# Eight of the 22 gate/value pairs of a gated MLP as seven half products each, with the splits of the early gated values moved back

## The chip, the cores and the metric

The kernel runs on one core of a Trainium2 chip. The metric is device time of the whole kernel in microseconds (us). The kernel before takes 888.9 us, the median of three runs (888.84 to 888.97).

Engines: TensorE (PE; PEld is its weight load) multiplies, VectorE (DVE) and ScalarE (ACT) work element by element, GpSimd (POOL) hardly takes part, SyncE (SP) issues most of the transfers. Each engine works off its own list of instructions in the order in which the built program holds them; semaphores hold an instruction back until what it needs is there.

## The reference, cut to what matters

One decoder layer over 528 tokens (16 meta tokens and 512 others), model width 1024. Two mixers read one normalised input through a common projection, their outputs go through an output projection, and a gated MLP with 2816 hidden channels follows. The change touches the MLP:

```python
def conv_glu_ffn(h, w_up, conv_w, conv_b, w_down):
    u = causal_dwconv(h @ w_up, conv_w, conv_b)      # width 3 over tokens
    gate, val = jnp.split(u, 2, axis=-1)             # 2816 channels each
    return (jax.nn.silu(gate) * val) @ w_down

h = h + conv_glu_ffn(rmsnorm(h, norm2_w[l]), ffn_w_up[l], ffn_conv_w[l], ffn_conv_b[l], ffn_w_down[l])
y = rmsnorm(h, final_norm_w)                         # the 16 meta tokens are dropped
```

## The kernel before

Everything lies channels by tokens: a tile has 128 channels on the partitions and the tokens along the free dimension. Of the meta tokens the MLP computes the last two alone, which the convolution needs, so a row has 514 tokens (14 to 528).

**Products.** All are made from two parts of each operand: `hi` is the operand rounded by an ACT copy to the type of the fast multiply, and `lo` is the rest, a DVE subtraction. A product takes three multiplies for each 128 rows of the contraction: hi by hi, hi by lo, lo by hi. `product` (line 190) does this for two token ranges, 14 to 272 and 272 to 528, so a tile `pup` of the up-projection (eight blocks of 128 rows) is 8 x 3 x 2 = 48 matmuls with 258 or 256 columns.

**Weights.** `chunks` is the list of all weight tiles in the order of use. `weights` hands out the next, and sees to it that the two behind it are under way: a transfer into `raw` by SP (line 169), the copy to `whi` by ACT (line 160), the subtraction to `wlo` by DVE (line 161). Of each of `raw`, `whi` and `wlo` there are three buffers, handed out as they come free. A tile has 1024 columns, eight blocks of 128.

**The gated part.** There are 22 pairs: gate tile j and value tile 22 + j. Each tile goes through `conv3`: product into a PSUM pair of banks (`banks2`, two of them), a DVE multiply by the norm factor `rstd2` (line 803, out of PSUM into `fr`), an ACT pass for the first tap with bias (line 805, `fc`), and two DVE passes for the other taps (line 807). Then come the silu of the gate (ACT, line 814), the DVE multiply of both (line 816), and at once the split of the gated value `ac` into `hi` (ACT, line 819) and `lo` (DVE, line 820). The norm factor is applied behind the product, so the product's right side `u2h`, `u2l` needs no norm and the first product can start early.

**The down product** comes after: eight output tiles `pdn`, one after the other, each over all 22 gated tiles (lines 829 to 831; 66 matmuls with 512 columns). The last one is done in two halves of 256 tokens, and the final norm and the stores follow it.

**What sets the order.** A scheduler places the instructions when the program is built, by data dependencies and by priorities: `first()` (weights) and `evac()` (what empties PSUM) raise the priority of what stands inside. `tc.issue_after(x)` holds work back until x is placed. All named buffers (`slot`) come from rings by tag.

Of the kernel before, what the change touches and what calls it, by code (L numbers as in the profile page):

```python
# [54 lines left out]
def tile_block(ctx: ExitStack, tc: tile.TileContext, xT, w_in, w_dt, w_out, w_up, w_down,  # L55
# [21 lines left out]
    def bank(name):  # L77
        return px.tile([P, 512], F32, tag="px", name=name)
# [20 lines left out]
    def col(c):  # L99
        return pt[:, c:c + 1]  # L100
# [43 lines left out]
        oorder += [(j, 1), (j, 0)]  # L144
    chunks += [(("out", j, s), w_out[j][:, s * KD * P:(s + 1) * KD * P], KD) for j, s in oorder]
    for j in range(KF):
        chunks += [(("up", j), w_up[j], KD), (("up", KF + j), w_up[KF + j], KD)]
    for j in range(KD):
        chunks += [(("dn", j, k0), w_down[j][:, k0 * P:(k0 + kc) * P], kc) for k0, kc in ((0, 8), (8, 8), (16, 6))]
    wdone = {}  # L150
    wnext = [0]

    def raw_tiles(key):
        name = "_".join(map(str, key))
        return (wp.tile([P, KD * P], F32, tag="raw", name=f"raw_{name}", bufs=3),
                wp.tile([P, KD * P], F32R, tag="whi", name=f"whi_{name}"),
                wp.tile([P, KD * P], F32R, tag="wlo", name=f"wlo_{name}"))

    def split_weights(raw, hi, lo, d, eng):
        A.activation(hi[:, d], raw[:, d], AF.Copy)  # L160
        eng.tensor_tensor(lo[:, d], raw[:, d], hi[:, d].bitcast(F32), ALU.subtract)  # L161

    def ahead(n):
        while wnext[0] < min(n, len(chunks)):
            key, src, kc = chunks[wnext[0]]
            with first():
# [14 lines left out]
    def product(groups, xh, xl, t0, nk, k0=0):  # L181


        for k in range(len(xh)):
            first, last = k0 + k == 0, k0 + k == nk - 1
            for ps, (hi, lo) in groups:
                wh, wl = hi[:, k * P:(k + 1) * P], lo[:, k * P:(k + 1) * P]
                for w, x, s, e in ((wh, xh[k], first, False), (wh, xl[k], False, False), (wl, xh[k], False, last)):
                    for a0, a1 in ((t0, HALF), (HALF, NT)):
                        PE.matmul(ps[:, O + a0:O + a1], w, x[:, a0:a1], start=s, stop=e)  # L190
# [602 lines left out]
        log_exp(rstd2, parts, T0, 1.0 / DM)  # L793


    def conv3(j):
        w = weights("up", j)
        ps = banks2(f"pup{j}")
        product([(ps, w)], u2h, u2l, T0, KD)
        if j == 0:  # L800
            second_norm()
        r = slot(f"fr{j}", tag="pr")
        V.tensor_tensor(r[:, T0:], ps[:, O + T0:O + NT], rstd2[:, T0:], ALU.mult)  # L803
        c = slot(f"fc{j}", 512, tag="pr")
        A.activation(c[:], r[:, META:], AF.Identity, bias=col(C_FB + j), scale=col(C_FW + 88 + j))  # L805
        for s in (1, 2):
            V.scalar_tensor_tensor(c[:], r[:, META - s:NT - s], col(C_FW + (2 - s) * 44 + j), c[:],  # L807
                                   ALU.mult, ALU.add)
        return c

    ah, al = [], []
    for j in range(KF):
        c = conv3(j)
        silu = A.activation(c[:], c[:], AF.Silu)
        c2 = conv3(KF + j)
        V.tensor_tensor(c2[:], c2[:], c[:], ALU.mult)
        tag = ["b0"] * 4 + ["b1"] * 4 + ["m"] * 8 + ["ab"] * 2 + ["fqv"] * 2 + ["bc"] * 2
        hi, lo = slot(f"ac{j}_hi", 512, F32R, tag=tag[j]), slot(f"ac{j}_lo", 512, F32R, tag=tag[j])
        A.activation(hi[:], c2[:], AF.Copy)
        V.tensor_tensor(lo[:], c2[:], hi[:].bitcast(F32), ALU.subtract)  # L820
        ah.append(hi)
        al.append(lo)

    def down(ps, ws, d):
        for (hi, lo), k0, kc in ws:
# [8 lines left out]
    acc = slot("facc", 512, tag="pr")  # L834
    with tc.issue_after(silu.ins):
        A.preload_act_table_set(LOGS)
    for j in range(KD):
        ws = [(weights("dn", j, k0), k0, kc) for k0, kc in ((0, 8), (8, 8), (16, 6))]
        hh = hs[j]
        sq = slot(f"fsq{j}", 512, tag="u") if j else acc  # L840
        if j < KD - 1:
            ps = bank(f"pdn{j}")
            down(ps[:], ws, slice(0, 512))
            V.tensor_tensor(hh[:, META:], hh[:, META:], ps[:], ALU.add)
            A.activation(sq[:], hh[:, META:], AF.Square)
            A.activation(hh[:, META:], hh[:, META:], AF.Copy, scale=col(C_FN + j))
            if j:
                V.tensor_tensor(acc[:], acc[:], sq[:], ALU.add)
            continue
        ps, halves = {}, (0, 256)  # L850
        for d0 in halves:
            d, dh = slice(d0, d0 + 256), slice(META + d0, META + d0 + 256)
            ps[d0] = bank(f"pdn{j}_{d0}")
            down(ps[d0][:, 0:256], ws, d)
        for d0 in halves:
            d, dh = slice(d0, d0 + 256), slice(META + d0, META + d0 + 256)
            with evac():
                V.tensor_tensor(hh[:, dh], hh[:, dh], ps[d0][:, 0:256], ALU.add)
# [3 lines left out]
                PE.matmul(p[:, 0:256], ones, acc[:, d], start=True, stop=False)  # L862
# [81 lines left out]
```

## Time and profile before

| | |
|---|---|
| median of three runs | 888.9 us (888.84 to 888.97) |
| the profiled execution's own time | 888.07 us |
| its span, first to last instruction | 886.3 us |
| granted TensorE clock, mean | 0.997 |
| busy in the span: PE, DVE, ACT | 870.5, 549.2, 418.4 us |
| matmuls | 6936 |

The page of the profile gives busy time by engine, the chain of work that ended last, and groups of equal instructions with count and mean duration. A duration of a pipelined instruction can overlap with the next, so the distance from one start to the next is read from the timeline. In rows such as `pup<-u2h,whi_up` the output stands ahead of the arrow and the inputs behind it; `xN` is a count.

### The profile page before, as it was taken

Reading aid. Unit: us, or ns where it says so; the run is one execution under the profiler, and the core shown is the slowest. Engines: PE = TensorE matmul, PEld = TensorE weight load, DVE = VectorE, ACT = ScalarE, POOL = GpSimd, SP = SyncE. Lnnn points to the kernel's source line nnn. Section 1 sums busy time; section 2 is a strip of 40 time slices with the busy share of each in tenths; the row PEclk is TensorE's granted clock in tenths of the full one; section 3 lists DMA queues with packets and bytes.
Section 4 is the critical chain, followed back from the end, with each engine's and each line's share of the span. In section 5 each row is a group of like instructions: output and inputs, shape, how many; then the busy total and the mean of one; then the engine's idle time right before and its main releaser. Section 6 shows DMA issues by size and latency. Waiting matters only on the chain.

```text
span 886.3 us, 16306 instructions
## 1 busy us (share of the span) xinstructions
PE 870.5 (98%) x6936; PEld 831.2 (94%) x6936; DVE 549.2 (62%) x885; ACT 418.4 (47%) x632; POOL 8.8 (1%) x30
## 2 busy tenths in 40 slices
PE   7999999999999999999999999999999999999995
PEld 6998898999999999999999999999999999888885
DVE  6985977788667766453333377767766667423333
ACT  8628885966445444453222354444444444323221
POOL 1000000000000000000000000000000000000001
PEclk9999999999999999999999999999999999999998
DMA  7234341221222322255322233332223333233312
GB/s 249 91 115 147 104 128 58 73 72 49 72 72 57 111 73 61 72 174 149 93 89 86 93 96 95 96 96 90 83 92 94 97 95 90 83 90 106 89 43 95
DMA packets 29081, 84.65 MB, mean 96 GB/s; under 512 B 3128, under 2 KB 6712, under 8 KB 29008
## 3 DMA queue, kind: packets, MB, share of 16 engines
q1 hardware_dynamic: 26480, 80.02, 29.0%
q10 hardware_dynamic: 2528, 3.60, 1.4%
q8 instruction: 54, 0.88, 0.4%
q14 instruction: 19, 0.16, 0.1%
HBM read 81.45 MB, written 2.15 MB: 94 GB/s over the span
## 4 chain that ended last, share of the span: by engine, by line
PE 95%; DMA 2%; ACT 1%; DVE 1%; issue 0%; SPq 0%; DVEq 0%
PE pj L190 32%; PE pup L190 28%; PE pout L190 10%; PE pdn L829 5%; PE pdn L830 5%; PE pdn L831 5%; PE psy L490 1%; PE psy L493 1%; DMA x<-in_xT_dram 1%; PE psu L447 1%; PE po L709 1%; PE po L708 1%; PE pa L692 1%; PE pS L680 1%; DMA rs_d<-rh 1%; PE psx L435 1%
## 5 line engine op out<-in xcount | busy, mean ns | idle before, releaser
L190 PE MATMUL pj<-u_lo,whi_in 128*128 128x272 f32 (+1 forms) x752 | 157.1, 288 | 0.0
L190 PE MATMUL pj<-u_hi,wlo_in 128*128 128x272 f32 (+1 forms) x752 | 156.3, 286 | 0.0
L190 PE MATMUL pj<-u_hi,whi_in 128*128 128x272 f32 (+1 forms) x752 | 155.3, 287 | 0.0
L190 PE MATMUL pup<-u2h,wlo_up 128*128 128x258 f32 x704 | 141.6, 282 | 0.0
L190 PE MATMUL pup<-u2h,whi_up 128*128 128x258 f32 x704 | 140.7, 282 | 0.0
L190 PE MATMUL pup<-u2l,whi_up 128*128 128x258 f32 x704 | 140.6, 281 | 0.0
L190 PEld LDWEIGHTS pj<-u_lo,whi_in 128*128 128x128 f32 x752 | 116.2, 188 | 2.4 <-issue 1.9
L190 PEld LDWEIGHTS pj<-u_hi,wlo_in 128*128 128x128 f32 x752 | 116.5, 189 | 2.0 <-issue 1.9
L190 PEld LDWEIGHTS pj<-u_hi,whi_in 128*128 128x128 f32 x752 | 115.5, 188 | 2.4 <-issue 2.3
L190 PEld LDWEIGHTS pup<-u2l,whi_up 128*128 128x128 f32 x704 | 108.1, 189 | 0.0
L190 PEld LDWEIGHTS pup<-u2h,wlo_up 128*128 128x128 f32 x704 | 108.0, 188 | 0.1
L190 PEld LDWEIGHTS pup<-u2h,whi_up 128*128 128x128 f32 x704 | 107.6, 188 | 0.0
L161 DVE TENSOR_TENSOR wlo_in<-raw_in,whi_in 128x1024 fp32r<-128x1024 f32 (+1 forms) x58 | 64.4, 1110 | 55.5 <-ACT whi_in L160 55.3
L160 ACT ACTIVATE whi_in<-raw_in 128x1024 fp32r<-128x1024 f32 (+1 forms) x58 | 56.0, 966 | 63.9 <-PE pj L190 59.2
L829 PE MATMUL pdn<-ac_hi,whi_dn 128*128 128x512 f32 (+1 forms) x198 | 73.2, 369 | 0.0
L830 PE MATMUL pdn<-ac_lo,whi_dn 128*128 128x512 f32 (+1 forms) x198 | 73.0, 369 | 0.0
L831 PE MATMUL pdn<-ac_hi,wlo_dn 128*128 128x512 f32 (+1 forms) x198 | 72.7, 367 | 0.0
L160 ACT ACTIVATE whi_up<-raw_up 128x1024 fp32r<-128x1024 f32 x44 | 46.7, 1061 | 49.1 <-PE pup L190 32.5
L807 DVE SCALAR_TENSOR_TENSOR fc<-fr,pt,fc 128x512 f32<-128x512 f32 x88 | 65.9, 749 | 2.4 <-ACT fc L805 0.9
L161 DVE TENSOR_TENSOR wlo_up<-raw_up,whi_up 128x1024 fp32r<-128x1024 f32 x44 | 53.9, 1226 | 14.8 <-ACT whi_up L160 14.8
L161 DVE TENSOR_TENSOR wlo_dn<-raw_dn,whi_dn 128x1024 fp32r<-128x1024 f32 (+1 forms) x24 | 27.3, 1137 | 57.4 <-ACT whi_dn L160 57.4
L803 DVE TENSOR_TENSOR fr<-pup,rstd 128x514 f32<-128x514 f32 x44 | 30.5, 693 | 47.7 <-PE pup L190 43.7
(293 smaller groups left out, 1414.5 us busy)
## 6 DMA issues: line engine op xcount, KB each, us to landing
raw_in<-in_w_in_dram SPq DMA_DIRECT2D x50, 512.0 KB, 3.6
raw_up<-in_w_up_dram SPq DMA_DIRECT2D x44, 512.0 KB, 3.6
raw_out<-in_w_out_dram SPq DMA_DIRECT2D x16, 512.0 KB, 3.8
raw_dn<-in_w_down_dram SPq DMA_DIRECT2D x16, 512.0 KB, 3.6
ab<-acum_d SPq DMA_DIRECT2D x16, 264.0 KB, 4.1
raw_dn<-in_w_down_dram SPq DMA_DIRECT2D x8, 384.0 KB, 3.1
rb<-rs_d SPq DMA_DIRECT2D x8, 257.0 KB, 4.4
xr<-in_xT_dram ACTq DMA_DIRECT2D x8, 257.0 KB, 3.3
```

The lines of the kernel that those rows point to most:

```text
L160: A.activation(hi[:, d], raw[:, d], AF.Copy)
L161: eng.tensor_tensor(lo[:, d], raw[:, d], hi[:, d].bitcast(F32), ALU.subtract)
L190: PE.matmul(ps[:, O + a0:O + a1], w, x[:, a0:a1], start=s, stop=e)
L435: PE.transpose(psx[0:n, t * P:(t + 1) * P], xs[t][:, a0:a1], ident)
L447: PE.matmul(psu[:], btk[0:n, b * P:(b + 1) * P], xdc[b][0:n, :], start=True, stop=True)
L490: PE.matmul(psy[q0:q0 + 64, a0 - META:a1 - META], xdt[b][:, hc], Ls[h][:, a0:a1], start=True, stop=False)
L493: PE.matmul(psy[q0:q0 + 64, a0 - META:a1 - META], ss[b - 1][:, hc], abs_[h][:, a0:a1], start=False, stop=True)
L803: V.tensor_tensor(r[:, T0:], ps[:, O + T0:O + NT], rstd2[:, T0:], ALU.mult)
L807: V.scalar_tensor_tensor(c[:], r[:, META - s:NT - s], col(C_FW + (2 - s) * 44 + j), c[:], ALU.mult, ALU.add)
L829: PE.matmul(ps, wh, xh, start=k0 + k == 0, stop=False)
L830: PE.matmul(ps, wh, xl, start=False, stop=False)
L831: PE.matmul(ps, wl, xh, start=False, stop=k0 + k == KF - 1)
```

## The change

`KINDS` gives each of the 22 pairs a kind.

- **U** (pairs 0 to 7) works as before: product of the tokens without norm, then the DVE multiply by `rstd2`.
- **N** (pairs 8, 10, 13, 15, 18, 21) takes normed tokens `nh`, `nl` as right side, with 48 matmuls for a tile as before. The DVE multiply out of PSUM falls away; the taps read PSUM themselves.
- **W** (pairs 9, 11, 12, 14, 16, 17, 19, 20) is Strassen's scheme in Winograd's form over a pair. The 2 x 2 blocks are gate and value by the two halves of the contraction (four blocks of 128 rows each), and on the other side the halves of the contraction by two token ranges, 14 to 272 and 270 to 528. In place of eight half products there are seven, with 4 x 3 = 12 matmuls of 258 columns each: 84 matmuls for a pair, where there were 96.

For W the weight sums are made on the chip (`scheme_weights`): a pair has three entries in `chunks`, `w0` (the gate tile as it is), `w2` (s1 and s2) and `w1` (two more sums; no transfer of its own, but it also makes and splits a fourth sum `s4` of 512 columns). The products `p1`, `p2`, `p6` go into single banks, `p75` and `p43` into the bank pairs. Seven DVE and ACT instructions then build gate `sg` and value `sv` (minus its sign, so its taps come from `ntap`), and the taps follow as before, 2 x 256 tokens at a time.

The normed tokens and their sums t1 to t4 are made by `normed_tokens` behind the gates of pairs 0 to 6 (`STEPS`). The gated value is kept whole in `ac` and split later (`SPLITS`): 0 to 8 behind the gates of pairs 7 to 20, 9 to 21 behind the gate of pair 21. The first two output tiles of the down product are computed side by side, and their weight tiles are fetched in that order.

```diff
+KINDS = "UUUUUUUUNWNWWNWNWWNWWN"
+STEPS = {0: (0, 1), 1: (2,), 2: (3,), 3: (4,), 4: (5,), 5: (6,), 6: (7,)}
+SPLITS = {7: (0,), 8: (1, 2), 10: (3,), 13: (4,), 15: (5,), 18: (6,), 20: (7, 8), 21: range(9, 22)}
+HT = 258
...
+        if KINDS[j] == "W":
+            chunks += [(("w0", j), w_up[j], KD), (("w2", j), w_up[KF + j], KD), (("w1", j), None, KD)]
...
+    chunks += [dn(j, *p) for p in PARTS for j in range(2)]
+    chunks += [dn(j, *p) for j in range(2, KD) for p in PARTS]
...
+    def split_half(x, hi, lo):
+        A.activation(hi, x, AF.Copy)
+        V.tensor_tensor(lo, x, hi.bitcast(F32), ALU.subtract)
+
+    def scheme_weights(key, src):
+        kind, j = key
+        if kind == "w0":
+            sums[j] = [raw_tile(key)]
+            nc.sync.dma_start(sums[j][0][:], src)
+            hi, lo = split_tiles(key)
+            split_weights(sums[j][0], hi, lo, slice(0, 2 * HK), V)
+            return hi, lo
+        if kind == "w2":
+            rg, rv = sums[j][0], raw_tile(key)
+            nc.sync.dma_start(rv[:], src)
+            s1, s2 = slot(f"s1_{j}", 512, tag="ab"), slot(f"s2_{j}", 512, tag="ab")
+            V.tensor_tensor(s1[:], rv[:, 0:HK], rv[:, HK:], ALU.add)
+            V.tensor_tensor(s2[:], s1[:], rg[:, 0:HK], ALU.add)
+            sums[j] += [rv, s2]
+            hi, lo = split_tiles(key)
+            split_half(s1[:], hi[:, 0:HK], lo[:, 0:HK])
+            split_half(s2[:], hi[:, HK:], lo[:, HK:])
+            return hi, lo
+        rg, rv, s2 = sums.pop(j)
+        V.tensor_tensor(rv[:, 0:HK], rv[:, 0:HK], rg[:, 0:HK], ALU.add)
+        V.tensor_tensor(rg[:, HK:], rg[:, HK:], s2[:], ALU.add)
+        hi, lo = split_tiles(key)
+        split_weights(rv, hi, lo, slice(0, 2 * HK), V)
+        h4, l4 = slot(f"s4h_{j}", 512, F32R, tag="ab"), slot(f"s4l_{j}", 512, F32R, tag="ab")
+        split_half(rg[:, HK:], h4[:], l4[:])
+        return hi, lo, h4, l4
...
+    def normed_tokens(i):
+        k = i // 2
+        if i % 2 == 0:
+            for kk in (k, k + KD // 2):
+                t = slot(f"n{kk}", tag="z")
+                V.scalar_tensor_tensor(t[:, T0:], hs[kk][:, T0:], col(C_N2 + kk), rstd2[:, T0:], ALU.mult, ALU.mult)
...
+                split_half(t[:, T0:], hi[:, T0:], lo[:, T0:])
...
+        V.tensor_tensor(t1, b11, b12, ALU.subtract)
+        V.scalar_tensor_tensor(t2, b22, -1.0, t1, ALU.mult, ALU.subtract)
+        V.tensor_tensor(t3, b22, b12, ALU.subtract)
+        V.scalar_tensor_tensor(t4, t2, -1.0, b21, ALU.mult, ALU.subtract)
+        for n, t in enumerate((t1, t2, t3, t4)):
+            d = slot(f"t{n + 1}_{k}", 2 * HT, F32R)
+            split_half(t, d[:, 0:HT], d[:, HT:])
...
+        hi, lo = weights("w0", j)
+        mul(p1, hi[:, 0:HK], lo[:, 0:HK], b11)
+        mul(p2, hi[:, HK:], lo[:, HK:], b21)
+        hi, lo = weights("w2", j)
+        mul(p6, hi[:, HK:], lo[:, HK:], t2)
+        mul(p75[:, 512:512 + HT], hi[:, 0:HK], lo[:, 0:HK], t1)
+        hi, lo, h4, l4 = weights("w1", j)
+        mul(p75[:, 0:HT], hi[:, 0:HK], lo[:, 0:HK], t3)
+        mul(p43[:, 512:512 + HT], h4, l4, b22)
+        mul(p43[:, 0:HT], hi[:, HK:], lo[:, HK:], t4)
+        with evac():
+            A.activation(sg[:, A_], p1, AF.Copy)
+            V.tensor_tensor(sv[:, A_], sg[:, A_], p6, ALU.add)
+            V.tensor_tensor(sg[:, A_], sg[:, A_], p2, ALU.add)
+            V.tensor_tensor(by_halves(su), sv[:, A_].unsqueeze(1).broadcast_to([P, 2, HT]), two(p75), ALU.add)
+            V.tensor_tensor(sv[:, B_], su[:, A_], p75[:, 512:512 + HT], ALU.add)
+            V.tensor_tensor(sv[:, A_], su[:, A_], p43[:, 0:HT], ALU.add)
+            V.tensor_tensor(sg[:, B_], su[:, B_], p43[:, 512:512 + HT], ALU.add)
...
+        for i in SPLITS.get(j, ()):
+            with tc.issue_after(gate.ins):
+                split_half(acs[i][:], hi[:], lo[:])
...
+    pdn = [bank(f"pdn{j}") for j in range(2)]
+    for k0, kc in PARTS:
+        w2 = [weights("dn", j, k0) for j in range(2)]
+        for k in range(kc):
+            for ps, (hi, lo) in zip(pdn, w2):
+                PE.matmul(ps[:], wh, ah[k0 + k][:], start=k0 + k == 0, stop=False)
+                PE.matmul(ps[:], wh, al[k0 + k][:], start=False, stop=False)
+                PE.matmul(ps[:], wl, ah[k0 + k][:], start=False, stop=k0 + k == KF - 1)
```

Three places of the built program, where the scheduler's order counts. The first is PE's list where pair 9 ends and pair 10 begins. Before, the last matmuls of value tile 31 (= 22 + 9) and the first of gate tile 10:

```order
L190 MATMUL pup31_7098<-u2l7_5864,whi_up_31_6965 128x256
L190 MATMUL pup31_7098<-u2h7_5863,wlo_up_31_6966 128x258
L190 MATMUL pup31_7098<-u2h7_5863,wlo_up_31_6966 128x256
L190 MATMUL pup10_7164<-u2h0_5086,whi_up_10_7031 128x258
L190 MATMUL pup10_7164<-u2h0_5086,whi_up_10_7031 128x256
```

The same place now, at the end of the seventh product of pair 9:

```order
L940 MATMUL p43_9_7145<-t4_3_6874,whi_w1_9_7153 128x258
L941 MATMUL p43_9_7145<-t4_3_6874,wlo_w1_9_7154 128x258
L939 MATMUL p1_11_7404<-n0_hi_6009,whi_w0_11_7275 128x258
L940 MATMUL p1_11_7404<-n0_lo_6010,whi_w0_11_7275 128x258
L939 MATMUL p2_11_7405<-n4_hi_6015,whi_w0_11_7275 128x258
L940 MATMUL p2_11_7405<-n4_lo_6016,whi_w0_11_7275 128x258
L250 MATMUL pup10_7279<-n0_hi_6009,whi_up_10_7186 128x258
```

Four matmuls of pair 11 now stand ahead of pair 10; they read `whi_w0_11`, which gets the buffer of `whi_w1_9`. Four matmuls of pair 19 stand ahead of pair 18 in the same way, and two of `pdn0` ahead of pair 21.

The second place is DVE's list where pair 17 (a W) ends. Before, pair 17 looked like every pair; this is pair 11's stretch, from the emptying of its gate tile on:

```order
L803 TENSOR_TENSOR fr11_7341<-pup11_7292,rstd2_5870 128x514
L161 TENSOR_TENSOR wlo_up_34_7350<-raw_up_34_7348,whi_up_34_7349 128x1024
L807 SCALAR_TENSOR_TENSOR fc11_7343<-fr11_7341,pt_75,fc11_7343 128x512 x2
L803 TENSOR_TENSOR fr33_7403<-pup33_7354,rstd2_5870 128x514
L161 TENSOR_TENSOR wlo_up_13_7416<-raw_up_13_7414,whi_up_13_7415 128x1024
L807 SCALAR_TENSOR_TENSOR fc33_7405<-fr33_7403,pt_75,fc33_7405 128x512 x2
L816 TENSOR_TENSOR fc33_7405<-fc33_7405,fc11_7343 128x512
```

Now, the end of pair 17:

```order
L966 TENSOR_TENSOR sv17_8212<-sg17_8211,p6_17_8208 128x258
L902 SCALAR_TENSOR_TENSOR fc38_8077<-sv16_8074,ntap_5871,fc38_8077 128x512
L179 TENSOR_TENSOR wlo_up_18_8252<-raw_up_18_8250,whi_up_18_8251 128x1024
L967 TENSOR_TENSOR sg17_8211<-sg17_8211,p2_17_8207 128x258
L988 TENSOR_TENSOR ac16_8204<-fc38_8077,fc16_8076 128x512
L179 TENSOR_TENSOR wlo_up_40_8282<-raw_up_40_8280,whi_up_40_8281 128x1024
L968 TENSOR_TENSOR su17_8213<-sv17_8212,p75_17_8209 128x516
L202 TENSOR_TENSOR s1_19_8400<-raw_w2_19_8398 128x512
L969 TENSOR_TENSOR sv17_8212<-su17_8213,p75_17_8209 128x258
```

The last instruction that reads `p75_17`, whose bank pair the next product `pup18` takes, stands behind two weight splits and behind `s1_19`, the first sum of a pair two further on, which waits for a transfer.

The third place is PE's list at the change to the down product. Now, around pair 21's first matmuls:

```order
L941 MATMUL p43_20_8611<-t4_3_6874,wlo_w1_20_8620 128x258
L1019 MATMUL pdn0_8922<-ac0_hi_7002,whi_dn_0_0_8748 128x512
L1020 MATMUL pdn0_8922<-ac0_lo_7003,whi_dn_0_0_8748 128x512
L250 MATMUL pup21_8753<-n0_hi_6009,whi_up_21_8652 128x258
L250 MATMUL pup21_8753<-n0_hi_6009,whi_up_21_8652 128x256
```

Two matmuls of the down product's first tile moved ahead of the last pair; they read `whi_dn_0_0`, which gets the buffer of `whi_w1_20`.

More of the change, by code (lines that the diff above doesn't have):

```diff
@@ L165, in ahead @@
             key, src, kc = chunks[wnext[0]]
+            if key[0] in ("w0", "w1", "w2"):
+                with first():
+                    wdone[key] = scheme_weights(key, src)
+                wnext[0] += 1
+                continue
             with first():
@@ L797, in conv3, with taps, at, taps_of @@
+    def taps(c, r, j, w, b):
+        n = c.shape[-1]
+        def at(s):
+            return r[..., 2 - s:2 - s + n] if len(r.shape) == 2 else r[:, :, 2 - s:2 - s + n]
+        A.activation(c, at(0), AF.Identity, bias=b, scale=w[2])
+        for s in (1, 2):
+            V.scalar_tensor_tensor(c, at(s), w[2 - s], c, ALU.mult, ALU.add)
+    def taps_of(j):
+        return [col(C_FW + i * 2 * KF + j) for i in range(3)]
+    def conv3(j, kind):
         w = weights("up", j)
         ps = banks2(f"pup{j}")
-        product([(ps, w)], u2h, u2l, T0, KD)
+        if kind == "U":
+            product([(ps, w)], u2h, u2l, T0, KD)
+        else:
+            product([(ps, w)], nh, nl, T0, KD)
@@ L800, in conv3 @@
         if j == 0:
             second_norm()
[L802 to L803 removed]
+        r = ps[:, O + T0:O + NT]
         c = slot(f"fc{j}", 512, tag="pr")
[L805 to L808, printed above, removed]
@@ L841, in tile_block @@
         if j < KD - 1:
-            ps = bank(f"pdn{j}")
-            down(ps[:], ws, slice(0, 512))
+            if j > 1:
+                ps = bank(f"pdn{j}")
+                down(ps[:], ws, slice(0, 512))
+            else:
+                ps = pdn[j]
             V.tensor_tensor(hh[:, META:], hh[:, META:], ps[:], ALU.add)
```

104 lines of the change are left out of this document (84 added, 20 removed).

## The prediction

> **What bounds the kernel now.** I read the page first, its busy times and the chain that ended last.
>
> ```profile
> span 886.3 us, 16306 instructions
> PE 870.5 (98%) x6936; PEld 831.2 (94%) x6936; DVE 549.2 (62%) x885; ACT 418.4 (47%) x632; POOL 8.8 (1%) x30
> PE 95%; DMA 2%; ACT 1%; DVE 1%; issue 0%; SPq 0%; DVEq 0%
> ```
>
> PE is the chain for 95% of the span. Next the chain in order of time from the gated part on (start, length, what), and the busy time by engine in that stretch (PE, PEld, DVE, ACT, POOL, then clock, DMA share, GB/s):
>
> ```profile
> 500.89 6.19 PE pup L190 x52
> 507.08 0.87 PE psn L791 x4
> 507.94 244.91 PE pup L190 x2060
> ...
> 867.61 0.86 PE psn L862 x4
> 508.00:752.85 244.85, 244.85 (x2061) 244.85 (x2060) 171.93 (x214) 111.51 (x136) 0.00 (x0) 1.00 0.30 93
> ```
>
> The 2112 matmuls of the gated part run without a hole to 752.85; 2060 in 244.91 us is 0.1189 us for each. So every matmul taken out there is worth 0.119 us, for as long as PE stays the last to be ready. DVE is busy 172 of 245 us, ACT 112. What fills them, by group (count | busy us, mean ns | idle before, released by):
>
> ```profile
> L807 DVE SCALAR_TENSOR_TENSOR fc<-fr,pt,fc 128x512 f32<-128x512 f32 x86 | 64.4, 749 | 2.4 <-ACT fc L805 0.9
> L161 DVE TENSOR_TENSOR wlo_up<-raw_up,whi_up 128x1024 fp32r<-128x1024 f32 x42 | 51.5, 1226 | 11.4 <-ACT whi_up L160 11.4
> L803 DVE TENSOR_TENSOR fr<-pup,rstd 128x514 f32<-128x514 f32 x44 | 30.5, 693 | 47.7 <-PE pup L190 43.7 <-ACT rstd L131 2.9
> L820 DVE TENSOR_TENSOR ac_lo<-fc,ac_hi 128x512 fp32r<-128x512 f32 x21 | 14.5, 692 | 14.1 <-ACT ac_hi L819 14.0
> L858 DVE TENSOR_TENSOR xr<-xr,pdn 128x256 f32<-128x256 f32 x2 | 0.8, 422 | 6.7 <-PE pdn L831 6.7
> L160 ACT ACTIVATE whi_up<-raw_up 128x1024 fp32r<-128x1024 f32 x42 | 44.6, 1061 | 40.9 <-PE pup L190 32.5 <-PE pout L190 4.6 <-issue 3.7
> L805 ACT ACTIVATE fc<-fr,pt 128x512 f32<-128x512 f32 x43 | 35.1, 816 | 1.1 <-DVE fr L803 1.1
> L814 ACT ACTIVATE fc<-fc 128x512 f32<-128x512 f32 x22 | 13.9, 632 | 41.3 <-DVE fc L807 41.3
> ```
>
> The weight copy on ACT waits 32.5 us for PE: it waits for a weight buffer that PE still reads. That wait is harmless while two other weight tiles are ready; it matters below.
>
> A row's duration is not what it costs in a queue. The timeline of DVE (start, length) shows starts closer together than the lengths, where an instruction does not read what the one ahead wrote:
>
> ```profile
> 330.36 0.69 DVE L642 TENSOR_TENSOR pp<-q,rq 128x512 f32<-128x512 f32 x1
> 330.97 0.68 DVE L645 TENSOR_TENSOR qS<-q,sd 128x512 f32<-128x512 f32 x1
> 331.57 0.55 DVE L646 TENSOR_TENSOR kS<-k,sd 128x384 f32<-128x384 f32 x1
> 332.03 0.42 DVE L656 TENSOR_TENSOR qBC<-q,sd 128x256 f32<-128x256 f32 x1
> 332.37 0.42 DVE L657 TENSOR_TENSOR kBC<-k,sd 128x256 f32<-128x256 f32 x1
> ...
> 639.61 1.23 DVE L161 TENSOR_TENSOR wlo_up<-raw_up,whi_up 128x1024 fp32r<-128x1024 f32 x1 [0.16 <-ACT whi_up L160]
> 640.76 1.53 DVE L807 SCALAR_TENSOR_TENSOR fc<-fr,pt,fc 128x512 f32<-128x512 f32 x2
> 642.32 0.69 DVE L816 TENSOR_TENSOR fc<-fc,fc 128x512 f32<-128x512 f32 x1
> ```
>
> Start to start: 0.60 for 512 elements (length 0.69), 0.34 for 256 (0.42), 1.15 for 1024 (1.23). Two taps that depend on each other take 1.56, so 0.78 each; two that don't I put at 0.75 - 0.08 = 0.67 (the 0.08 is what the others gain).
>
> **What is removed.** A W pair has 84 matmuls for 96, so 8 x 12 = 96 fewer: 96 x 0.1189 = 11.4 us off PE. The 672 left in W pairs have 258 columns where the mean was 257: 672 x 0.1189 / 257 = 0.3 back. Net 11.1. N and U pairs and the down product keep their matmuls.
>
> **What DVE gets.** No transfer is added or taken away (`w1` has none); SP's list only follows the new order. The three small products for `ntap` stand among the first instructions of the kernel, on a DVE that waits for transfers there. Tile by tile, for a W pair: four sums of 512, three splits of 512 (two in w2, one in s4), two splits of 1024, five TT (tensor-tensor instructions) of 258 and one of 516 out of PSUM, four taps (two and two alternate, 0.70 on the mean) and the gate product: 7 x 0.60 + 2 x 1.15 + 5 x 0.34 + 0.61 + 4 x 0.70 + 0.60 = **12.2 us**. PE takes 84 x 0.119 = 10.0 for it. An N pair has no `fr`: 2 x 1.15 + 4 x 0.72 + 0.60 = **5.8 us** (PE 11.4). Each late split adds 0.60. The operand forms with 2 x 258 and a repeated input are in no row of before; I take them by L803 and L858, which also read PSUM, since size is all that sets those lengths. The lowest price is these starts; the highest the full lengths (rivals).
>
> So the work comes in four blocks, each from an N pair to the W ahead of the next N: 10-12, 13-14, 15-17, 18-20. DVE against PE: 5.8 + 2 x 12.2 + 0.6 = 30.8 against 31.4 us; 18.6 against 21.4 for 13-14. DVE fits, with 2% to spare in three blocks of four, and ACT (about 7 us for a W by L160, L805, L814 and halves of them) with more. The point where lateness counts is the end of a block: N's first product needs the bank pair of `p75`, which was full only 2.9 us earlier (the 24 matmuls of `p43`).
>
> **The U part.** The norming of the tokens adds 2 x (0.67 + 0.60) or 4 x 0.34 + 4 x 0.34 for a step, 2.5 to 2.7 us. By the order a pair has 9 to 13 us of DVE work against 11.4, about 79 against 91 over pairs 0 to 7. A product may be emptied 5.7 us late before PE stops, since two bank pairs alternate. Taken as 0; if that cover were gone, the worst pair (0 to 1, some 2 us over) would cost 2.
>
> **Waits at the ends of blocks**, by walking the queues with the starts above:
>
> - Pairs 9 to 10, and 20 to 21. The hoisted matmuls need a `whi` whose buffer PE frees with its last matmul of the pair; behind it comes the ACT copy of 1024. How such a copy and its reader follow each other:
>
> ```profile
> 644.23 1.06 ACT L160 ACTIVATE whi_up<-raw_up 128x1024 fp32r<-128x1024 f32 x1 [0.55 <-PE pup L190]
> 645.32 1.23 DVE L161 TENSOR_TENSOR wlo_up<-raw_up,whi_up 128x1024 fp32r<-128x1024 f32 x1 [0.16 <-ACT whi_up L160]
> ```
>
> 1.06 and some 0.1 for the two hand-overs: 1.2 us each, with the whole next product queued behind. 2.4 together. (DVE alone would hold pair 10 up for 0.4, inside this.)
> - Pairs 12 to 13. The taps of pair 11 wait for an ACT queue that first copies `p1_12`, which is done 72 matmuls, 8.6 us, before the block's end, at 22.8. The copy of 258 (0.4, taken as two thirds of L814's 512) and the tap pass (0.8) end at 24.1 with the hand-over. From there DVE has four taps, two splits of 1024, two TT of 258, the gate product, `su` and the reader of `p75_12` left: 4 x 0.67 + 2 x 1.15 + 2 x 0.34 + 0.60 + 0.61 + 0.42 = 7.3, so 31.5, and 31.6 for PE, against 31.4: 0.2.
> - Pairs 14 to 15 and 17 to 18. `s1` of a later pair stands ahead of that reader and waits for its weights, whose raw buffer came free with the split `wlo_up_15` (17.1 us into a block of 21.4) or `wlo_up_18` (28.5 of 31.4). The transfer takes 3.6 us from issue to landing:
>
> ```profile
> raw_up<-in_w_up_dram SPq DMA_DIRECT2D x44, 512.0 KB, 3.6
> ```
>
> 17.1 + 3.7 + 0.6 + 0.5 = 21.9, so 0.6 late; 28.5 + 3.7 + 0.6 + 0.4 = 33.2, so 1.8 late (the hoist of `p1_19`, 1.2, lies inside).
>
> Sum of the waits: 2.4 + 0.2 + 0.6 + 1.8 = **5.0 us**. Lower bound 0, upper bound 14 (the second rival).
>
> **The hand-over to the down product.** It starts with tiles 0 to 8, which are split by then. The two output tiles side by side take 6 x 0.218 = 1.3 us for each gated tile (0.218: 114.8 us from 752.85 to 867.61 for 528 matmuls of 512 columns, the last tile's 132 halves counted as 66). Tile 9 is needed 11.7 us after the last up-matmul. DVE and ACT have its split about 5.4 us after it (one ACT tap pass, two taps, gate, split), then one split each 0.65. The weight tile `dn_1_8` can only come when PE has freed a buffer, but PE's list has 16 matmuls of `pdn0` (3.5 us) in that place. Taken as 0; with the cover gone it is a copy and a split, 1.06 + 1.23 = 2.3.
>
> **Sum.** 888.07 - 11.1 + 5.0 = 882.0 for a profiled execution; that one lay 0.8 under the median, so **882.8 us**, 0.7% faster.
>
> **Rivals.**
>
> *Nothing waits.* PE's list keeps going because the hoists find their weights. For it: PE never stood still for a weight in the stretch above. Against: there a copy had two further tiles as cover; here the buffer is read by the matmul just ahead. 888.9 - 11.1 = 877.8.
>
> *DVE becomes the bound: slower.* Place: the three blocks with two W. If each DVE instruction costs its full length there, a W has 7 x 0.69 + 2 x 1.23 + 5 x 0.42 + 0.69 + 4 x 0.75 + 0.69 = 13.8 us, an N 6.2, a block 34.5 against 31.4: 3 x 3.1 = 9.3 lost. Waits for ACT and transfers inside DVE's queue then add to the time instead of hiding (0.5 a block, 2.0), the first boundary 1.3, and the late gate of pair 21 and the down weights some 2: 14.6, so 888.9 - 11.1 + 14.6 = 892.4. It decides from some 0.08 us more for each of the 46 instructions of a block. Against it stand the starts 0.60 apart; for it, that most instructions in the new order wait for another engine, and a waiting one gains nothing from the overlap.
> A rule of the Trainium skill speaks for this rival (VectorE: DVE Perf Modes, section "The DRAIN you can't avoid"): after each operation the pipe is flushed, and the next does not start until it is empty. By that rule the blocks would go by full lengths, and the sum would be 892.4. The trace differs as far as it goes: 512 elements start 0.60 apart with rows of 0.69.
>
> *The raw buffers are the bound.* A W holds two of the three raw buffers until its last sums, so each W's second transfer starts late. If it lands 0.6 us later than 3.6 at each of eight W pairs, with a DVE queue that stands still, 5 us more: 888. For it, the two boundaries above; against, that 16 engines are at a 0.30 share.
>
> **Chances.** Forecast, with waits of 2 to 8 us (880 to 886): 0.58. Nothing waits: 0.08. Raw buffers or other waits of 8 to 12 us (886 to 890): 0.20. DVE bound: 0.14. A measurement here tells some 0.2% (1.8 us) from no change: faster means under 887.1, slower over 890.7. Faster: 0.58 + 0.08 + 0.08 of the 0.20 = 0.74. Same: the other 0.12 and 0.02 of the DVE case = 0.14. Slower: 0.12. The range 879.5 to 890.5 leaves out about 0.06 below and 0.12 above. Since few of the cases are slower, no second range is needed; the forecast's own is 880 to 886.
>
> **What would show it.** Right: 6840 matmuls; PE idle of 1 to 2 us at the five block ends and none inside; gated part of 251.9 - 11.1 + 5.0 = about 246 us; PE waits there named by `whi_w0`, `whi_dn` or `p75`. Wrong: PE idle in every W pair with DVE at over 95% busy between pairs 9 and 20 (DVE bound); holes on DVE ahead of `s1` behind a transfer (raw buffers); PE idle between 752 and 765 (hand-over); idle in U pairs.

## The result

The changed kernel takes **882.15 us** in the median of four runs (882.03 to 883.05), the kernel before 888.87 us (888.73 to 888.97). The ratio is 0.9929, with a 95% interval from 0.9918 to 0.9941: 0.7% faster. The forecast was 882.8 us.

The profiled execution of the changed kernel is the slowest of its four, 883.05 us. Its totals, and the shares of the chain that ended last:

```profile
span 880.9 us, 16283 instructions
PE 861.5 (98%) x6840; PEld 821.5 (93%) x6840; DVE 596.4 (68%) x1012; ACT 438.7 (50%) x688; POOL 8.9 (1%) x30
PE 96%; ACT 1%; DMA 1%; DVE 1%; issue 1%; DVEq 0%; SPq 0%; ACTq 0%
```

There are 96 matmuls fewer and 127 DVE instructions more. PE is busy 9.0 us less and the span is 5.4 us shorter, so PE now stands still for longer than it did. The waits of PE at the ends of W pairs, by what ended them (us in total, times, longest), and the two stretches that matter (PE, PEld, DVE, ACT, POOL, clock, DMA share, GB/s):

```profile
PE p L939 <- ACT whi_w L178: 2.1, 2, 1.1
PE pdn L1019 <- ACT whi_dn L178: 1.1, 1, 1.1
```

```profile
501.76:748.10 246.34, 243.16 (x2025) 242.11 (x2024) 216.05 (x331) 130.35 (x186) 0.00 (x0) 1.00 0.31 94
600.00:746.00 146.00, 142.82 (x1185) 141.88 (x1184) 132.25 (x203) 75.82 (x108) 0.00 (x0) 1.00 0.33 99
```

The gated part lasts 246.3 us. Where the pairs of kind W lie, DVE is busy 91% of the time (132.25 of 146.00), and PE misses 3.2 us of the stretch. The chain of waits shows where those lie (start, length, what):

```profile
508.98 96.56 PE pup L250 x812
615.52 1.06 ACT whi_w L178
617.38 11.42 PE pup L250 x96
648.50 11.56 PE pup L250 x96
670.17 11.62 PE pup L250 x96
701.91 1.07 ACT whi_w L178
703.76 11.42 PE pup L250 x96
734.87 1.07 ACT whi_dn L178
736.71 11.42 PE pup L250 x96
```

The 812 matmuls ahead of the first scheme pair run without a hole. Three times the chain goes through an ACT copy of about 1.06 us, at the ends of pairs 9, 17 and 20, and in each case the matmuls behind it are hoisted ones of a later product. One of them in the timelines of PE, ACT and DVE:

```profile
701.66 0.28 PE L941 MATMUL p<-t,wlo_w 128*128 128x258 f32 x1
703.02 0.38 PE L939 MATMUL p<-n_hi,whi_w 128*128 128x258 f32 x1 [1.08 <-ACT whi_w L178]
...
701.91 1.06 ACT L178 ACTIVATE whi_w<-raw_w 128x1024 fp32r<-128x1024 f32 x1 [3.26 <-PE p L940]
...
702.24 0.69 DVE L202 TENSOR_TENSOR s<-raw_w 128x512 f32<-128x512 f32 x1 [0.87 <-DMA raw_w<-in_w_up_dram]
702.85 0.42 DVE L969 TENSOR_TENSOR sv<-su,p 128x258 f32<-128x258 f32 x1
```

PE's last matmul of pair 17 starts at 701.66. The copy for the hoisted product waits for the buffer that this pair still reads, and PE starts again at 703.02, so 1.24 us are lost beside the usual 0.12. At the same time DVE stood still for 0.87 us ahead of the first weight sum of pair 19 (L202), whose transfer had not landed, with the reader of the bank `p75` (L969) queued behind it. That reader ended at 703.27: a second wait beside the first. It cost nothing here, since the first matmul of `pup18`, which needs that bank, stands behind the four hoisted ones and started at 703.60.

### The profile page after: what moved, and what is told of

It is laid out like the page before. It is cut to its first block, busy times and chain, and to the rows that moved or that the text cites. A ratio compares the mean times of both kernels' runs of the same rounds, so it can differ in the third digit from the quotient of the medians.

```text
span 880.9 us, 16283 instructions
## 1 busy us (share of the span) xinstructions
PE 861.5 (98%) x6840; PEld 821.5 (93%) x6840; DVE 596.4 (68%) x1012; ACT 438.7 (50%) x688; POOL 8.9 (1%) x30
## 4 chain that ended last, share of the span: by engine, by line
PE 96%; ACT 1%; DMA 1%; DVE 1%; issue 1%; DVEq 0%; SPq 0%; ACTq 0%
PE pj L250 33%; PE pup L250 18%; PE pout L250 10%; PE pdn L1006 3%; PE pdn L1007 3%; PE pdn L1005 3%; PE p L939 3%; PE p L940 3%; PE p L941 3%; PE pdn L1019 1%; PE pdn L1021 1%; PE pdn L1020 1%; PE psy L550 1%; DMA x<-in_xT_dram 1%; PE psy L553 1%; PE pa L752 1%
## 5 line engine op out<-in xcount | busy, mean ns | idle before, releaser
L178 ACT ACTIVATE whi_dn<-raw_dn 128x1024 fp32r<-128x1024 f32 (+1 forms) x24 | 23.6, 987 | 73.8 <-PE pdn L1006 53.4
L1006 PE MATMUL pdn<-ac_lo,whi_dn 128*128 128x512 f32 (+1 forms) x154 | 55.9, 363 | 0.0
L1005 PE MATMUL pdn<-ac_hi,whi_dn 128*128 128x512 f32 (+1 forms) x154 | 55.6, 361 | 0.0
L250 PE MATMUL pup<-u2h,wlo_up 128*128 128x258 f32 (+1 forms) x256 | 51.6, 283 | 0.0
L250 PE MATMUL pup<-u2l,whi_up 128*128 128x258 f32 (+1 forms) x256 | 51.1, 281 | 0.0
L250 PE MATMUL pup<-u2h,whi_up 128*128 128x258 f32 (+1 forms) x256 | 51.1, 282 | 0.0
L179 DVE TENSOR_TENSOR wlo_up<-raw_up,whi_up 128x1024 fp32r<-128x1024 f32 x28 | 34.2, 1220 | 9.8 <-ACT whi_up L178 9.7
L179 DVE TENSOR_TENSOR wlo_out<-raw_out,whi_out 128x1024 fp32r<-128x1024 f32 x16 | 19.6, 1225 | 30.1 <-ACT whi_out L178 30.1
L250 PEld LDWEIGHTS pup<-u2h,wlo_up 128*128 128x128 f32 x256 | 39.3, 188 | 0.1
L250 PEld LDWEIGHTS pup<-u2l,whi_up 128*128 128x128 f32 x256 | 39.3, 189 | 0.0
```

The source lines that it names most:

```text
L1005: PE.matmul(ps, wh, xh, start=k0 + k == 0, stop=False)
L1006: PE.matmul(ps, wh, xl, start=False, stop=False)
```

## The account of PE

Each kernel below can be followed by one sum. I take the stretch from the start of the last `psn` matmul ahead of the gated part to the start of the last `pdn` matmul, so that the work upstream, which differs by up to 2 us between single executions, is left out. The kernel before has 368.71 us there. A pair of kind W takes off 12 matmuls of 0.1189 us, and its 84 matmuls, all of 258 columns, start 0.1201 us apart (164 from 628.64 to 648.22 in the changed kernel), which gives 84 x 0.0012 = 0.10 us back: 1.33 us net. The waits are what PE's starts lie apart beyond 0.119 us, wherever they are over 0.19 apart; starts at a lower clock are in it. In the four kernels where two matmuls of `pdn0` still stand ahead of pair 21 (changed, e3, e7, e11), 0.2 us of it is no wait: these two have 512 columns and take 0.22 us each.

| kernel | W pairs | median us | ratio, 95% | waits us | 368.71 - 1.33 a pair + waits | stretch measured |
|---|---|---|---|---|---|---|
| before | 0 | 888.87 | | 0 | 368.7 | 368.71 |
| changed | 8 | 882.15 | 0.9918 to 0.9941 | 4.44 | 362.5 | 362.37 |
| all N (e6) | 0 | 888.65 | 0.9992 to 1.001 | 0 | 368.7 | 368.71 |
| no hoist (e1) | 8 | 882.65 | 0.9922 to 0.9952 | 4.61 | 362.7 | 362.64 |
| first sum held (e11) | 8 | 883.90 | 0.9938 to 0.9963 | 5.51 | 363.6 | 363.30 |
| no hoist, first sum held (e2) | 8 | 880.48 | 0.9893 to 0.9923 | 2.47 | 360.5 | 360.43 |
| the same and late taps (e9) | 8 | 880.19 | 0.9893 to 0.9920 | 2.56 | 360.6 | 360.58 |
| late taps alone (e3) | 8 | 882.68 | 0.9919 to 0.9944 | 4.45 | 362.5 | 362.37 |
| no hoist, 1 DVE add a pair (e4) | 8 | 883.07 | 0.9925 to 0.9955 | 5.60 | 363.7 | 363.64 |
| no hoist, 3 DVE adds a pair (e5) | 8 | 896.23 | 1.0065 to 1.0099 | 18.78 | 376.8 | 376.84 |
| eleven W (e7) | 11 | 893.18 | 1.0034 to 1.0062 | 19.83 | 373.9 | 373.82 |
| e9 with nine W, one early | 9 | 883.63 | 0.9928 to 0.9955 | 7.35 | 364.1 | 363.90 |
| e9 with nine W, three in a row | 9 | 882.49 | 0.9917 to 0.9947 | 5.57 | 362.3 | 362.52 |

Sum and measurement agree within 0.3 us in all of them. This is bookkeeping: the excess of the starts is read from the same trace as the stretch. What it tests is the 1.33 us of a W pair, and that no other loss lies in the stretch. So two things make the difference between these kernels: the number of matmuls, and how far PE's starts are held up, nearly always at the ends of W pairs (in e7 inside them too, and in e5, e7 and one of e10 by a lower clock as well). The experiments ask what sets that second number.

## The experiments

**The side parts alone (e6).** The scheme is not used; the normed tokens, the splits behind gates, the side by side start of the down product and the negated taps stay.

```diff
-KINDS = "UUUUUUUUNWNWWNWNWWNWWN"
+KINDS = "UUUUUUUUNNNNNNNNNNNNNN"
```

> All fourteen pairs 8 to 21 with the products of the kernel before (no pair by the scheme), with the rest of the change left in: the gated values split behind gates, the negated taps at the start. 96 matmuls come back, so by the prediction's sum the time is before + 0.3 = 888.8 us, and PE has no wait over 0.2 us at the ends of pairs 9, 12, 14, 17 and 20. If the side parts of the change cost more than the forecast gave them, 889.5 or more; if moving the splits of the gated values is worth time by itself, 888.0 or less.

Measured: 888.65 us, ratio 1.0001 (0.9992 to 1.001), and no wait of PE in the stretch. The moved splits and the normed products are worth nothing and cost nothing; DVE has room for them. In the stretch that took 132.25 us of DVE above, it needs:

```profile
600.00:746.00 146.00, 146.00 (x1230) 146.00 (x1229) 81.14 (x98) 54.70 (x69) 0.00 (x0) 1.00 0.31 94
```

**The hoists (e1).** Theory: the matmuls that the scheduler hoists ahead of an ordinary product, behind a weight copy, cost PE 1.2 us at three places. The edit holds them behind the last matmul of the pair before:

```diff
+        with tc.issue_after(last[0].ins):
             mul(p1, hi[:, 0:HK], lo[:, 0:HK], b11)
             mul(p2, hi[:, HK:], lo[:, HK:], b21)
...
+                with tc.issue_after(last[0].ins):
                     PE.matmul(ps[:], wh, ah[k0 + k][:], start=k0 + k == 0, stop=False)
```

> The change with one thing undone: the four matmuls of pairs 11 and 19 and the two of the down product that the scheduler had put ahead of pairs 10, 18 and 21 stay in their place behind those pairs. My theory (three waits of 1.2 us for a weight copy behind a matmul just ahead): at pairs 9 to 10 the 1.3 us wait falls to about 0.4 (the last reader of p75_9 ends 0.4 us after the last matmul of pair 9), at 20 to 21 from 1.3 to about 0.1; at 17 to 18 nothing is won, since the last reader of p75_17 ends 1.6 us after PE is done. Together 1.9 us: 880.2. Rival, DVE as the bound: the waits only change their name, 881.8 to 882.3. Rival, all three waits vanish: 878.5.

Measured: 882.65 us, no gain. The waits of PE of this kernel (`sv L971` is the reader of `p75`, `L969` in the changed kernel), and DVE at the end of pair 12:

```profile
PE pup L251 <- DVE sv L971: 3.5, 3, 1.7
```

```profile
647.33 0.69 DVE L970 TENSOR_TENSOR su<-sv,p 128x516 f32<-128x516 f32 x1
648.88 0.69 DVE L202 TENSOR_TENSOR s<-raw_w 128x512 f32<-128x512 f32 x1 [0.86 <-DMA raw_w<-in_w_up_dram]
649.49 0.41 DVE L971 TENSOR_TENSOR sv<-su,p 128x258 f32<-128x258 f32 x1
```

The copies no longer stop PE. The waits at the ends of pairs 9 and 20 fell as expected (1.19 to 0.48 and 1.24 to 0.18 beside the usual 0.12), but others came in their place. At the ends of pairs 12 and 17 PE's starts lie 1.75 and 1.96 us apart (0.20 and 1.36 before the edit), since the order of DVE moved as well: now the first sum of pair 14 stands ahead of the reader at the end of pair 12 and waits 0.86 us there for its transfer. My 880.2 was wrong, because it took DVE's order as given: the edit moved a stalled sum to a place where there had been no wait.

**Both, and the first sum alone (e2, e11).** The second edit holds the first weight sum of a pair behind the reader of `p75` of the W pair before it:

```diff
+                if emptied[0] is not None:
+                    st.enter_context(tc.issue_after(emptied[0]))
                 V.tensor_tensor(s1[:], rv[:, 0:HK], rv[:, HK:], ALU.add)
...
-            V.tensor_tensor(sv[:, B_], su[:, A_], p75[:, 512:512 + HT], ALU.add)
+            emptied[0] = V.tensor_tensor(sv[:, B_], su[:, A_], p75[:, 512:512 + HT], ALU.add).ins
```

> As the kernel without the hoists, and in addition the first sum s1 of a W pair is placed on DVE only behind the last reader of the p75 ahead of it, so that its wait for the weight transfer holds up nothing else. My theory (the wait at pairs 17 to 18 is s1's transfer, 0.9 us of DVE idle, and what follows it): another 1.3 us, 878.9, with 0.5 us of waits at block ends in all. Rival, the raw buffers are the bound: s1 and what hangs on it comes later still, and PE waits for w2 instead inside the W pairs: 880 or above.

> The changed kernel with the first weight sum held behind the first reader of the last bank of the pair before; the hoisted matmuls stay. Theory (the three hoists cost PE 1.3 us each whatever VectorE does, as their copy comes behind the last matmul of the pair): 882.2, no gain, PE's waits still named by the weight copies. Rival (the stalled sum was what held the ends of the blocks up, and the second run's gain came from it alone): 880.5.

Measured: 880.48 us with both. The theory had 878.9 with 0.5 us of waits; 2.5 us are left, and none of it inside a W pair, where the rival had put it. The second alone takes 883.90 us, which is no gain (its interval reaches that of the changed kernel). PE's waits in the stretch, first with both, then with the second alone:

```profile
PE pup L255 <- DVE sv L975: 1.7, 3, 0.6
```

```profile
PE p L943 <- ACT whi_w L178: 2.1, 2, 1.1
PE pdn L1023 <- ACT whi_dn L178: 1.1, 1, 1.1
PE p L945 <- DVE wlo_w L179: 0.5, 1, 0.5
PE pup L254 <- DVE sv L973: 0.2, 1, 0.2
```

By place (distance of PE's starts at the end of the pair, less 0.12):

| end of pair | changed | no hoist (e1) | first sum held (e11) | both (e2) |
|---|---|---|---|---|
| 9 | 1.19 | 0.48 | 0 | 0 |
| 12 | 0.08 | 1.63 | 1.19 | 0.63 |
| 14 | 0.12 | 0.11 | 0.33 | 0 |
| 17 | 1.24 | 1.84 | 1.24 | 0.75 |
| 20 | 1.24 | 0.18 | 1.24 | 0.78 |

At the end of pair 17 each of the two causes hides the other: the stalled sum alone leaves a wait of 1.84 us, the copy alone 1.24, and only without both does it fall to 0.75. At the other ends the single edits gained nothing for another reason: the scheduler made a new order. In e1 the stalled sum of pair 14 moved ahead of the reader at the end of pair 12; in e11 the hoist left the end of pair 9 and came up at the end of pair 12, with 0.7 us more behind it for the split of the same weights. Both edits together take the waits from 4.4 to 2.5 us. What is left is the wait for the reader of `p75` itself, 0.6 to 0.8 us at the ends of pairs 12, 17 and 20, with no transfer ahead of it. A tap pass of an earlier tile stands between it and the instruction ahead of it in the evacuation, and takes 0.67 us of DVE; no run moves that pass (DVE at the end of pair 17, with both edits):

```profile
698.96 0.69 DVE L974 TENSOR_TENSOR su<-sv,p 128x516 f32<-128x516 f32 x1
699.56 0.75 DVE L907 SCALAR_TENSOR_TENSOR fc<-sv,ntap,fc 128x512 f32<-128x512 f32 x1
700.23 0.42 DVE L975 TENSOR_TENSOR sv<-su,p 128x258 f32<-128x258 f32 x1
```

**How full DVE is (e4, e5).** On top of e1, one or three DVE additions of 512 elements that nothing needs are made in each W pair:

```diff
             V.tensor_tensor(sg[:, B_], su[:, B_], p43[:, 512:512 + HT], ALU.add)
+            for _ in range(3):
+                V.tensor_tensor(su[:, 0:512], sg[:, 0:512], sv[:, 0:512], ALU.add)
```

> As the kernel without the hoists, with one more DVE addition of 512 elements (0.60 us from start to start; its result is not used) in each W pair, right behind the emptying of the products. My theory, 30.8 us of DVE work against 31.4 of PE in three blocks and 18.6 against 21.4 in one: one addition makes 32.0, so about 0.6 us lost in three blocks, 1.8 us over the kernel without hoists (882.0). DVE as the bound: each of the eight counts in full, 4.8 us more (885.0). DVE with much room: no change (880.2).

> The same with three additions in each W pair. My theory: a block has 34.4 us of DVE work against 31.4, three blocks lose 3.0 each, the block of pairs 13 and 14 (20.4 against 21.4) nothing: 9 us over the kernel without hoists (889.2). DVE as the bound: 24 x 0.6 = 14.4 us more (894.6). DVE with much room: under 3 us (883).

Measured: 883.07 us with one. That is not told apart from e1's 882.65; in the traces the waits rise by 1.0 us (5.60 against 4.61), where the theory had 1.8. With three it is 896.23 us, more than any of the three theories gave. What an added instruction costs in DVE's queue, and PE's waits:

```profile
641.99 0.68 DVE L975 TENSOR_TENSOR su<-sg,sv 128x512 f32<-128x512 f32 x1
642.60 0.41 DVE L968 TENSOR_TENSOR sv<-sg,p 128x258 f32<-128x258 f32 x1
642.93 0.74 DVE L903 SCALAR_TENSOR_TENSOR fc<-sg,pt,fc 128x512 f32<-128x512 f32 x1
643.59 0.74 DVE L903 SCALAR_TENSOR_TENSOR fc<-sv,ntap,fc 128x512 f32<-128x512 f32 x1
644.25 0.68 DVE L975 TENSOR_TENSOR su<-sg,sv 128x512 f32<-128x512 f32 x1
```

```profile
PE pup L251 <- DVE sv L971: 11.2, 4, 4.2
```

The addition is 0.68 us long and the next starts 0.61 us after it; the readers of PSUM start 0.33 and the taps 0.66 us apart. Those are the prices of the forecast. Three blocks at 30.8 + 2 x 3 x 0.60 = 34.4 us of DVE against 31.4 of PE should lose 9.0 us; the idle time of PE at the ends of the blocks came to 12.0 us against 4.2 in e1, so 7.8 more. (Where PE ran slower, DVE had more time, so 7.8 is not a clean test of the 9.0.) The rest of the excess, 6.8 us, is no wait at all: with each wait of 3 us or more PE's clock fell. In e5 the windows that begin with those three waits' ends:

```profile
615.20:618.00 2.80, 2.80 (x24) 2.80 (x24) 2.80 (x6) 2.08 (x3) 0.00 (x0) 1.00 0.38 149
651.15:653.86 2.71, 2.71 (x12) 2.71 (x13) 2.71 (x6) 1.52 (x2) 0.00 (x0) 0.50 0.03 6
710.02:714.90 4.88, 4.88 (x23) 4.88 (x24) 4.88 (x10) 2.15 (x3) 0.00 (x0) 0.50 0.00 0
747.06:753.00 5.94, 5.94 (x28) 5.94 (x29) 5.77 (x10) 2.67 (x4) 0.00 (x0) 0.50 0.29 88
```

Behind a wait of 0.60 (the first row) the clock is 1.00 and 24 matmuls start in 2.80 us. Behind starts 4.44, 4.28 and 3.04 us apart it is 0.50, and 12 matmuls start in 2.71 us. Half of 2.71 + 4.88 + 5.94 is 6.8 us. The windows end up to 0.6 us ahead of the clock's rise, so the agreement is good to some 0.5 us.

**More W pairs (e7, and e10 on top of e9).** Eleven in two long rows; nine with one at the end of the first part; nine with three in a row:

```diff
-KINDS = "UUUUUUUUNWNWWNWNWWNWWN"
+KINDS = "UUUUUUUUNWWWWWNWWWWWWN"    (e7)
+KINDS = "UUUUUUUUWWNWWNWWNWWNWN"    (e10, early)
+KINDS = "UUUUUUUUNWWNWWNWWNWWWN"    (e10, late)
```

> Eleven pairs by the scheme instead of eight (9 to 13 and 15 to 20), 36 more matmuls off: 4.3 us more off PE. Theory (VectorE is nearly full in a block of scheme pairs, 12.2 us for a pair against 10.0 of PE): the two blocks need 67.4 and 79.6 us of VectorE against 61.4 and 71.4 of PE, so PE waits about 14 us in all; 888.5 - 15.7 + 0.3 + 14.2 = 887.3, and up to 892 if the waits are over 3 us each and the granted clock falls to half after them as it did in the run with three more additions. If VectorE is not what sets the end of a block: 888.5 - 15.7 + 5.1 = 877.9.

> On top of the three edits, nine pairs by the scheme in blocks of two with one ordinary pair between (8, 9, 11, 12, 14, 15, 17, 18 and 20): 12 more matmuls off, 1.4 us by the mean, 1.3 by the 0.1201 us that a matmul of 258 columns takes. Theory (a block of two scheme pairs and an ordinary one just fits VectorE, 30.8 us against 31.4): 880.2 - 1.3 + one more end of a block at 0.8 = about 879.7, if pair 8 finds its weight sums ready at the end of the first part. Rival (VectorE has no room left): more than 882, with waits inside the pairs.

> On top of the three edits, nine pairs by the scheme (9, 10, 12, 13, 15, 16, 18, 19 and 20): the last block has three of them in a row. Theory (three in a row need 5.8 + 3 x 12.2 + 0.6 = 43.0 us of VectorE against 41.4 of PE): that block waits some 1.6 us more, so 880.2 - 1.3 + 1.6 = 880.5. Rival (VectorE does not set the ends of the blocks): 878.9.

Measured: 893.18, 883.63 and 882.49 us, where I had expected 887.3 (up to 892), 879.7 and 880.5; all three are slower than the eight pairs that they start from. For e7, PE's waits and the stretch:

```profile
PE p L939 <- ACT whi_w L185: 4.8, 4, 1.6
PE p L941 <- DVE s4l L186: 2.9, 2, 1.6
PE p L939 <- DVE sv L969: 2.5, 5, 0.8
```

```profile
600.00:757.00 157.00, 143.02 (x1144) 139.66 (x1143) 149.59 (x241) 81.00 (x120) 0.00 (x0) 0.99 0.31 92
```

DVE is busy 95% of the stretch and PE waits inside the pairs: this is what the slower rival of the prediction was to look like, here by more work for DVE and not by a higher price of an instruction. The waits are some 18 us where I had 14.2, and one stretch at a lower clock is added. In e10 late the third W pair in a row costs 3.0 us more waits than e9 (1.6 expected), in e10 early the end of pair 9 alone makes PE's starts lie 3.31 us apart, with the lower clock behind it. In that wait DVE is busy all the time:

```profile
614.16:617.47 3.31, 0.28 (x4) 0.10 (x2) 3.31 (x6) 1.06 (x1) 0.00 (x0) 1.00 0.50 139
```

It is also busy for the whole of the 14.16 us ahead of it (from 600.00), so there nothing but its own work held it up, and it has no room for a ninth pair. In e10 late it is busy 31.53 of the 31.70 us from 703.30 to the block's end at 735.00, but 2.10 us of idle time behind an ACT copy lie just ahead of 703.30; how much of the 3.0 us comes from that, the runs don't separate.

**The negated taps (e3, e9).** They are made behind the gate of pair 1 instead of at the start.

> The three negations of the taps are made behind the gate of pair 1 instead of ahead of the first work. Theory (they stand in VectorE's list ahead of v_lo at the start, and PE's first products come 0.5 us later): 0.5 us less than the changed kernel, 881.7. If the negations are hidden as the prediction said: 882.2.

> The hoisted matmuls held behind the previous pair, the first weight sum held behind the first reader of the last bank of the pair before, and the negated taps made behind the gate of pair 1. By the sum of the runs so far: 880.5 - 0.5 = 880.0; if the negations cost nothing 880.5; if the gain of the second edit was chance, 882.

Measured: 882.68 us (no gain) and 880.19 us (the same as e2). I had taken them for the reason that the first products of the profiled execution come 0.5 us later. The chain at the start says what it was, in the kernel before and in the changed one:

```profile
5.29 4.12 DMA x<-in_xT_dram
```

```profile
5.30 4.62 DMA x<-in_xT_dram
```

A transfer that both kernels have took 0.5 us longer in that execution. The negations are hidden, as the prediction said.

e2 and e9 are the best versions of all: 0.9908 and 0.9907 of the time before (0.9893 to 0.9920 for e9), 1.7 to 2.0 us below the changed kernel. Their intervals touch that of the changed kernel (from 0.9918), but the slowest run of both (881.32) is below its fastest (882.03), and the waits in the traces are 2 us less.

## Why the prediction was right

**The bound.** Every matmul taken out was worth its distance while PE was the last to be ready; the account above closes within 0.3 us. The net of the matmuls was forecast at 11.1 us and is 8 x 1.33 = 10.6: matmuls of 258 columns lie 0.1201 us apart, not 0.1189 x 258 / 257 = 0.1194. That term was mis-sized by 0.5.

**Waits at the block ends.** None lay inside a pair, and those at pairs 9, 17 and 20 were where they were put. The forecast's sign, 1 to 2 us of PE idle at all five ends, held at these three alone; at pairs 12 and 14 there was next to none. Their sizes, measured as the distance of starts less 0.12:

| end of pair | forecast | measured | released by |
|---|---|---|---|
| 9 | 1.2 | 1.19 | copy of the hoisted product |
| 12 | 0.2 | 0.08 | |
| 14 | 0.6 | 0.12 | |
| 17 | 1.8 | 1.24 | copy; the stalled first sum beside it |
| 20 | 1.2 | 1.24 | copy for the down product |

With 0.6 us for the first matmuls behind a wait, which start 0.19 to 0.24 us apart, the waits are 4.4 us; the forecast had 5.0. Where the forecast was too high is the transfer of the first sum: the step "17.1 + 3.7 + 0.6 + 0.5 = 21.9, so 0.6 late" did not occur at the end of pair 14, and at the end of pair 17 the sum did wait (0.87 us), but PE's next matmuls were the hoisted ones, which the copy held; when they were through, the reader behind the sum had ended. The two misses, 0.5 too much gain and 0.6 too much waiting, took each other back. That is luck in part. Of the 5.0 us of waiting, the 2.4 at pairs 9 and 20 came out right in size and for the reason given; the 1.8 at pair 17 was given to the late transfer, with the hoist inside it, and it was the other way round; the 0.6 at pair 14 did not come. That the late transfer is real shows in e1, where it costs 1.84 us at pair 17 once the hoist is gone.

**The first part and the hand-over.** Taken as 0, and they are: 812 matmuls without a hole, and PE goes from the last up product into the down product at 748.12 with the starts of a normal sequence. The stretch from there to the last `pdn` is not longer than before (122.9 us against 123.4, of which 0.4 are the two matmuls done ahead of pair 21).

**The rivals.** *Nothing waits* (877.8) did not happen; the nearest that any run came is 880.2, with 2.6 us of waits left. *Raw buffers* (888) was wrong as a bound, but its mechanism is in DVE's waits in the changed kernel between pairs 9 and 21: three times ahead of a first sum, 2.2 us in all.

```profile
DVE s L202 <- DMA raw_w<-in_w_up_dram: 2.2, 3, 1.0
```

*DVE becomes the bound* (892.4) is wrong for this change and right close beside it: one more W pair is enough to lose against eight, and three more, or 1.8 us more of DVE in each, are enough to be slower than the kernel before. Its place was named rightly. Its size, 0.08 us more for each of 46 instructions of a block (3.7 us), is what e5 added (3.6 us more, slower than before); with a third of that, in e4 (1.2 us more in a block), 1.0 us was lost in all. The paragraph of the Trainium skill that spoke for it (VectorE: DVE Perf Modes, section "The DRAIN you can't avoid") also says that a next operation that is not held starts earlier, and the forecast had told its first half alone. The traces agree with that second half for instructions that don't need each other's results: 0.68 us long, 0.61 from start to start, in a queue that was never empty.

## What to carry to other kernels

A saving on the bounding engine is worth its full price only as far as the next engine keeps up in every single block: here the means (DVE busy 68% of the span) say nothing, and the ratio of DVE to PE work from one empty bank to the next (30.8 against 31.4 us) decides. When a wait has two causes that lie side by side, as at the end of pair 17, the profile names one alone; take both away before saying that either costs nothing. A scheduler's order changes with each edit, so the first thing to read after one is where the waits have gone, not whether the named one has left.

## What the runs showed of the hardware

**The clock falls with a wait of about 3 us.** PE ran at a granted clock of 0.50 for 2.7 to 5.9 us behind starts that lay 3.04 to 4.44 us apart in e5, and at 0.58 on the mean of 2.5 us behind 3.31 us in e10 early. It stayed at 1.00 behind 1.90 us (the longest distance in e7). Behind 1.96 us in e1 it did not change either; that execution is recorded at 0.95 from end to end, with matmuls no further apart than elsewhere (675 starts in 80 us). In e7 it fell without such a wait, after two of 1.36 and 1.29 us close together (windows of that kernel):

```profile
660.70:664.00 3.30, 1.21 (x8) 0.82 (x7) 3.01 (x6) 1.06 (x1) 0.00 (x0) 1.00 0.53 144
664.00:666.00 2.00, 2.00 (x11) 2.00 (x12) 2.00 (x4) 1.52 (x2) 0.00 (x0) 0.56 0.34 137
666.00:668.00 2.00, 2.00 (x13) 2.00 (x12) 2.00 (x5) 0.00 (x0) 0.00 (x0) 0.59 0.00 0
668.00:670.00 2.00, 2.00 (x19) 2.00 (x19) 2.00 (x5) 0.63 (x1) 0.00 (x0) 1.00 0.00 0
```

PE was busy 1.21 of 3.30 us, and the next 4 us ran at little over half the clock. The Trainium skill (TensorE: Matmul & The Clock Gate, section "What's actually happening") says that PE falls to half its clock after an idle window of some 3.4 us. The traces agree with the half, but not with a full idle window: in e5 a wait of 2.76 us was enough, and the recorded clock fell within it, at 746.26, 1.96 us after the last matmul's end at 744.30; in e7 a window that was idle for most of its length was enough. The records of the clock at half speed last 3.41 us (three times) or 6.83 us (twice) in e5, e7 and e10 early. A wait of 3 us so cost some 1.4 to 3 us more than itself in e5 (half of 2.7 to 5.9), which the forecast's upper bound had left out.

**Columns.** Matmuls of 258 columns lie 0.1201 us apart (163 distances in the changed kernel), while an ordinary product, half of 256 and half of 258, takes 11.42 us for 96: 0.1190.
